# A two-layer trunk in split precision: modulation chunks in two buffer slots, an earlier gate, two more seven-product pairs

## The chip, the cores and the metric

The kernel runs on one core of one Trainium2 chip. Its time is the device time of one execution in microseconds; the median of three runs counts. Separately, the hardware profiler took one execution; all views of the profile below come from that one. The engines are called by their short names: PE is TensorE, DVE VectorE, ACT ScalarE, POOL GpSimd, SP the engine whose queue issues the loads.

## The reference

Two layers work on a latent stream of 256 tokens and a context stream of 256 tokens, both 1024 wide, with shared weights. All is float32.

```
for i in range(2):
    ml = split(silu(c)     @ w_ada[i] + b_ada[i], 9)   # shift, scale, gate for three sub-layers
    mc = split(silu(c_ctx) @ w_ada[i] + b_ada[i], 9)
    x = x + 0.5 * g1 * swiglu(modulate(rmsnorm(x, norm_w[0]), sh1, sc1), w_ffn1_in, w_ffn1_out)
    x = x + g2 * token_mixer(modulate(rmsnorm(x, norm_w[1]), sh2, sc2))
    x = x + 0.5 * g3 * swiglu(modulate(rmsnorm(x, norm_w[2]), sh3, sc3), w_ffn2_in, w_ffn2_out)
return rmsnorm(x_latent, final_norm_w)

swiglu(h, w_i, w_o) = (silu(h @ w_i[:, :2816]) * (h @ w_i[:, 2816:])) @ w_o
modulate(h, shift, scale) = h * (1 + scale) + shift
```

`x` stands for both streams, each with its own modulation (`ml` or `mc`). The token mixer projects once into 1952 columns, runs latent attention with 8 heads on one part and a gated convolution of width 3 on the other, and projects the two back together. In the second layer the context stream is needed only as keys and values, so that everything after that layer's mixer, and the last modulation vectors (5 to 8), are for the latent stream alone.

## The kernel before

**Number format.** Each matrix product is made of three PE products (`mm3`, L228, L229, L230): high part of the weight by high part of the data, high by low, low by high. A weight arrives as a 512 KB load into `wraw` (three buffers). ACT casts it to the high part `whi` (L234), DVE subtracts that from the raw weight to get the low part `wlo` (L235); each has five buffers. Products accumulate in four PSUM buffers named `mm`; four more, tag `psn`, serve norms and special sums.

**Residual and norm.** `X` holds both streams transposed, features on partitions, 8 blocks of 128 features by 512 tokens. An output projection (`into_x`) makes eight blocks: each ends with a DVE operation that adds the gated product to `X` (L347), ACT squares the new `X` (L280) and DVE adds that to `acc` (L284). The first five blocks take both streams in one 512-column product, the last three take each stream apart, so that the norm of the context stream can start while the latent stream is still being made. The norm is a chain: PE sums `acc` over partitions (`psn_s`, L244), DVE adds epsilon, POOL takes the power, PE spreads the result over partitions (`psn_r`, L252), DVE multiplies into `t` (L302), and `h` comes out as a high part on ACT (L303) and a low part on DVE (L304). Before the last FFN, PE covers this chain with products on `ax`, the not yet normalised data; those products go to `psf` and `mm` and are scaled afterwards.

**FFN.** 2816 hidden features are 22 pairs (one gate tile and one up tile of 128 features), run as two halves of 11 pairs, each half followed by its output projection. A regular pair (`gated`) is 48 matmuls of 512 columns. A fast pair (`gated_fast`) makes the same two products with seven instead of eight block products, in 84 matmuls of 256 columns, and needs more additions on DVE before and after. `FAST` lists the fast pairs of the first, second and third FFN. The fourth FFN (`ffn_end`) has the latent stream alone, turns the output around (tokens on partitions), and multiplies its output weights by the gate as they arrive (`wload(..., by=gb)`, L213). For that, the gate vector has to lie along the free dimension, the same on all partitions: `spread` (L532, L534) lets PE broadcast it with eight small matmuls and ACT copy it to `gb`.

**Modulation.** The modulation vectors are 18 products of a vector by a 1024 × 1024 matrix. They are not made on PE (but for the first two): the matrix is cut in chunks of 128 outputs, SP loads a chunk `wa` of 512 KB, and one DVE operation per stream multiplies it by the activated condition and sums along the row (L175), writing the products, which nobody needs, to `junk`. 128 chunks make 224 such operations. `wa` and `junk` live in pool `g`, with three slots of 512 KB, which `gb`, the fast pairs' `fg` and some mixer tiles use too. The chunks stand in a queue. `ada(n, after)` adds n to an account and issues one chunk for each whole unit; `PACE` has, for each of the first three FFNs, the n per pair and the n per joint output block. `ada_until(d, m)` issues whatever is still missing up to vector m of layer d.

**Order.** The kernel is written with a tile framework that works out a static order of all instructions on each engine from a planner's timeline, and waits between engines by semaphores. A small edit therefore moves instructions in places that the diff doesn't name. Loads go through SP in one queue.

The mixer interleaves the attention's heads with the convolution's projections; the head outputs `o` are split into `mixa` (two heads to a tile), the convolution's into `mixc`, and the output projection takes `mixc` first, the `mixa` of the last heads last.

Of the kernel before, what the change touches and what calls it, by code (L numbers as in the profile page):

```python
# [18 lines left out]
P = 128  # L19
# [3 lines left out]
TT = 2 * T  # L23
# [32 lines left out]
LEAD = 1  # L56
EARLY_AT = (1, 1, 2, 2, 3, 3)
NT1 = 3
PACE = ((0.85, 1.75), (0.8, 1.7), (0.9, 1.75))
MIX_PACE = 0  # L60
FAST = ((8, 10, 13, 15, 17, 19), (6, 8, 10, 13, 15, 17, 19), (6, 8, 10, 13, 15, 17, 19))


@with_exitstack
def tile_kernel(ctx: ExitStack, tc: tile.TileContext, xT, ctxT, cT, cR, w_ada, b_ada, norm_w,
                f1i, f1o, f2i, f2o, f2r, w_in, qn_w, kvn_w, w_uq, w_ukv, conv_w, w_out, fin_w,
                qtab, out):
    nc = tc.nc
# [35 lines left out]
    ident = const.tile([P, P], F32, name="ident")  # L104
# [64 lines left out]
    def ada_chunk(d, m, ct):  # L169
        wt = slot("g", "wa")  # L170
        load(wt, w_ada[d, m, ct])
        md = mods[d][m]
        for s in needed(d, m):
            junk = slot("g", "junk")
            nc.vector.scalar_tensor_tensor(junk, wt, 1.0, scb[:, s, :], ALU.mult, ALU.mult,  # L175
                                           accum_out=md[:, s, ct:ct + 1])
        if ct == NKT - 1:
            for s in needed(d, m):
                nc.vector.tensor_tensor(md[:, s, :], md[:, s, :], ba[:, d, m, :], ALU.add)
                if m % 3 == 1:  # L180
                    nc.vector.scalar_tensor_tensor(md[:, s, :], md[:, s, :], 1.0, nw[:, d, m // 3, :],
                                                   ALU.add, ALU.mult)
                if m in (2, 8):
                    nc.vector.tensor_scalar_mul(md[:, s, :], md[:, s, :], 0.5)
# [329 lines left out]

            into_x(d, gate, streams, lambda i: wo[d, half, i], hid, nxt if half else None, pace)

    def ffn_end(d, wi, wr, gate, nrm):


        ada_until(d, gate)  # L520
        parts = [(tt, h) for tt in range(2) for h in range(2)]
        gb = slot("g", "gb")
        fwb = slot("g", "fwb")
        load(fwb, fin_w.broadcast_to([P, D]))
        xt, acc = {}, {}

        def spread(h, after):

            ps = mmtile((0, TT))
            for k in range(4):  # L530
                with tc.issue_after(after.ins):
                    nc.tensor.matmul(ps[:, k * P:(k + 1) * P], mod(d, gate, 1, 4 * h + k).broadcast_to([P, P]), ident,  # L532
                                     start=True, stop=True)
            nc.scalar.copy(gb[:, h * TT:(h + 1) * TT], ps)  # L534

        def turn_x(part, tag, after):
            tt, h = part
# [17 lines left out]
        hid, w = {}, {}  # L555
        for j in range(NPAIR):
            hid[j], end = gated(d, wi, j, nrm, [1])
            if j == 1:
                for h in range(2):
                    spread(h, last_mm[0])  # L560
            if j == 2:
                for part in parts:
                    acc[part] = psn.tile([P, TT], F32, tag="psn", name="pse")
            if 6 <= j < 9:
                turn_x(parts[j - 6], ("cv", "cv", "qf")[j - 6], last_mm[0])
            k = j - LAG
            if 0 <= j - 1:
                w[j - 1] = wload(wr[j - 1], WCH, by=gb)
            if 0 <= k < NPAIR - TAIL:
                for part in parts:  # L570
                    gather(part, k, hid[k], w[k])
# [33 lines left out]
    def mixer(d, H, last, nxt):  # L605
# [212 lines left out]
                attend(*units[i - 2], st2.pop(i - 2))  # L818
        for _ in steps:
            pass  # L820

        pooled[0] = False
        ada_until(d, 5)
        order = (4, 5, 6, 7, 0, 1, 2, 3)
        into_x(d, 5, qs, lambda i: w_out[d, i], [MIX[k] for k in order], nxt, (0, 0 if last else MIX_PACE))


    ends = {}
# [43 lines left out]
    for d in range(DEPTH):  # L872
# [2 lines left out]
        ffn(d, f1i, f1o, 2, prev, [0, 1], nrm, PACE[2 * d], FAST[2 * d])  # L875
        qs = [1] if last else [0, 1]
        H, nrm = nrm.H, Norm(d, 2, qs)
        mixer(d, H, last, nrm)
        prev, nrm = nrm, None if last else Norm(d + 1, 0, qs)
        if last:  # L880
            ffn_end(d, f2i, f2r, 8, prev)
        else:
            ffn(d, f2i, f2o, 8, prev, qs, nrm, PACE[1], FAST[1])

# [78 lines left out]
```

## Time and profile before

| | |
|---|---|
| median of three runs | 1666.20 us (1666.19 to 1667.68) |
| profiled execution's own time | 1667.98 us |
| its span in the trace | 1666.2 us |
| mean granted PE clock | 0.993 |
| PE busy | 1620.8 us, 97% |
| DVE busy | 1233.5 us, 74% |
| ACT busy | 681.0 us, 41% |
| read from HBM | 246.28 MB, 148 GB/s over the span |

How to read the views quoted below. A row of a timeline has its start in us from the start of the span, its duration, the engine, the source line, the operation, the tile written and the tiles read, the shape, how many instructions the row joins, and in brackets how long the engine had been idle and what ended that. A row of a table of stretches has the stretch, its length, the busy time and number of instructions for PE, PE's weight loads, DVE, ACT and POOL, the granted PE clock, the busy share of the DMA engines and their GB/s. A row of the waits has the waiting engine, tile and line, an arrow to what it waited for, the sum of the idle time, how many times, and the longest. A row of the groups has line, engine, operation, tiles, shape and count, then the busy time and mean ns of one, then the idle time ahead of them and what ended most of it. A row of the loads has the tiles, the queue, the count, the size and the median us from issue to landing. The stages lie so: the start and the first FFN to 390 us, first mixer to 607 us, second FFN to 966 us, the second layer's FFN to 1340 us, last mixer to 1465 us, last FFN to the end.

### The profile page before, as it was taken

How to read it: one execution, taken by the hardware profiler on the slowest of the kernel's cores; microseconds unless marked ns; L12 is line 12 of the kernel's file. 1: busy time of each engine (PE TensorE's matmuls, PEld its weight loads, DVE VectorE, ACT ScalarE, POOL GpSimd, SP SyncE). 2: the span in 40 equal slices, each digit the busy share in tenths (PEclk: the TensorE clock that was granted, in tenths of full speed). 3: DMA queues.
4: the chain of work that ended last, by engine and by line, in shares of the span. 5: the costliest groups of instructions: out<-in, count | busy, mean ns of one | idle time of the engine just before them, and what ended most of it. 6: DMA issues, size and time to landing. Idle time of an engine off the chain costs nothing.

```text
span 1666.2 us, 24512 instructions
## 1 busy us (share of the span) xinstructions
PE 1620.8 (97%) x9605; PEld 1418.5 (85%) x9605; DVE 1233.5 (74%) x2049; ACT 681.0 (41%) x1097; POOL 58.1 (3%) x65
## 2 busy tenths in 40 slices
PE   6999999999999999999999999999999999999998
PEld 5889888888877688888898888988998998989997
DVE  5597788787477778878887779876675578766665
ACT  4433224323476354331243244331343257744443
POOL 0000000001111000000000000000000011100000
PEclk9999999999999999999999999999999999999999
DMA  9335555553222333346445533456345333345653
GB/s 374 134 114 164 190 168 160 171 180 100 74 75 71 126 102 114 128 163 203 152 142 186 166 106 113 149 198 230 127 152 196 116 97 126 119 143 182 189 168 123
DMA packets 73363, 249.70 MB, mean 150 GB/s; under 512 B 8736, under 2 KB 12960, under 8 KB 73248
## 3 DMA queue, kind: packets, MB, share of 16 engines
q1 hardware_dynamic: 72960, 247.62, 45.1%
q8 instruction: 75, 1.23, 0.3%
q10 hardware_dynamic: 288, 0.52, 0.1%
q14 instruction: 40, 0.33, 0.1%
HBM read 246.28 MB, written 1.05 MB: 148 GB/s over the span
## 4 chain that ended last, share of the span: by engine, by line
PE 79%; DMA 9%; DVE 7%; issue 3%; ACT 2%; SPq 0%; POOL 0%; DVEq 0%; POOLq 0%; ACTq 0%
PE mm L228 21%; PE mm L229 21%; PE mm L230 21%; DMA wa<-in_w_ada 6%; DMA wraw<-in_f2r 2%; DVE junk L175 2%; DVE wlo L235 2%; PE psg L228 2%; PE psg L230 2%; PE psg L229 2%; PE pso L784 1%; PE pst L771 1%; PE pse L228 1%; PE pse L229 1%; PE pse L230 1%
## 5 line engine op out<-in xcount | busy, mean ns | idle before, releaser
L234 ACT CAST whi<-wraw 128x1024 fp32r<-128x1024 f32 (+1 forms) x345 | 350.8, 1022 | 636.6 <-PE mm L229 341.7
L228 PE MATMUL mm<-h,whi 128*128 128x256 f32 (+1 forms) x1488 | 504.5, 343 | 5.1 <-ACT whi L234 3.1
L229 PE MATMUL mm<-h,whi 128*128 128x256 f32 (+1 forms) x1488 | 503.8, 340 | 4.1 <-DVE h L304 3.8
L230 PE MATMUL mm<-h,wlo 128*128 128x256 f32 (+1 forms) x1488 | 502.7, 339 | 0.1
L235 DVE TENSOR_TENSOR wlo<-wraw,whi 128x1024 fp32r<-128x1024 f32 (+1 forms) x345 | 408.8, 1190 | 112.9 <-ACT whi L234 105.8
L228 PEld LDWEIGHTS mm<-h,whi 128*128 128x128 f32 x1488 | 281.3, 191 | 43.4 <-issue 7.3
L175 DVE SCALAR_TENSOR_TENSOR junk<-wa,scb 128x1024 f32<-128x1024 f32 x224 | 267.1, 1223 | 63.0 <-DMA wa<-in_w_ada 62.0
L229 PEld LDWEIGHTS mm<-h,whi 128*128 128x128 f32 x1488 | 283.6, 191 | 35.2 <-DVE h L304 5.4
L230 PEld LDWEIGHTS mm<-h,wlo 128*128 128x128 f32 x1488 | 283.5, 191 | 30.5 <-DVE wlo L235 0.3
L230 PE MATMUL mm<-hid,wlo 128*128 128x512 f32 (+1 forms) x627 | 224.4, 358 | 0.0
L229 PE MATMUL mm<-hid,whi 128*128 128x512 f32 (+1 forms) x627 | 224.2, 358 | 0.0
L228 PE MATMUL mm<-hid,whi 128*128 128x512 f32 (+1 forms) x627 | 223.1, 358 | 0.0
L229 PEld LDWEIGHTS mm<-hid,whi 128*128 128x128 f32 x627 | 120.0, 191 | 16.7
L228 PEld LDWEIGHTS mm<-hid,whi 128*128 128x128 f32 x627 | 120.0, 191 | 16.7
L230 PEld LDWEIGHTS mm<-hid,wlo 128*128 128x128 f32 x627 | 119.9, 191 | 16.6
L347 DVE SCALAR_TENSOR_TENSOR X<-mm,mod,X 128x256 f32<-128x256 f32 x120 | 53.4, 478 | 38.5 <-PE mm L230 38.1
L234 ACT CAST hid<-sg 128x512 fp32r<-128x512 f32 (+1 forms) x88 | 49.0, 561 | 47.3 <-DVE sg L386 30.5
L213 DVE TENSOR_TENSOR wraw<-wraw,gb 128x1024 f32<-128x1024 f32 x22 | 26.9, 1224 | 49.8 <-DMA wraw<-in_f2r 47.0
L235 DVE TENSOR_TENSOR hid<-sg,hid 128x512 fp32r<-128x512 f32 (+1 forms) x88 | 54.0, 613 | 10.1 <-ACT hid L234 10.1
L280 ACT ACTIVATE sq<-X 128x256 f32<-128x256 f32 x63 | 25.4, 414 | 86.3 <-DVE X L347 80.2
L222 POOL TENSOR_TENSOR wlo<-wraw,whi 128x512 fp32r<-128x512 f32 x18 | 25.1, 1414 | 794.0 <-ACT whi L219 794.0
L386 DVE TENSOR_TENSOR sg<-sg,mm 128x512 f32<-128x512 f32 (+1 forms) x65 | 38.0, 584 | 18.5 <-PE mm L230 18.2
(236 smaller groups left out, 2213.5 us busy)
## 6 DMA issues: line engine op xcount, KB each, us to landing
wa<-in_w_ada SPq DMA_DIRECT2D x128, 512.0 KB, 4.0
wraw<-in_f1i SPq DMA_DIRECT2D x88, 512.0 KB, 3.6
wraw<-in_f2i SPq DMA_DIRECT2D x88, 512.0 KB, 4.0
wraw<-in_f1o SPq DMA_DIRECT2D x44, 512.0 KB, 3.8
wraw<-in_w_in SPq DMA_DIRECT2D x32, 512.0 KB, 3.5
wraw<-in_f2o SPq DMA_DIRECT2D x22, 512.0 KB, 3.6
wraw<-in_f2r SPq DMA_DIRECT2D x22, 512.0 KB, 4.6
waf<-in_w_ada SPq DMA_DIRECT2D x16, 512.0 KB, 8.2
```

Of the source, the lines that this page charges most:

```text
L175: nc.vector.scalar_tensor_tensor(junk, wt, 1.0, scb[:, s, :], ALU.mult, ALU.mult, accum_out=md[:, s, ct:ct + 1])
L213: nc.vector.tensor_tensor(raw, raw, by, ALU.mult)
L222: nc.gpsimd.tensor_tensor(w[1][:, c], raw[:, c], f32(w[0][:, c]), ALU.subtract)
L228: nc.tensor.matmul(ps, w[0], x[0], start=start, stop=False)
L229: nc.tensor.matmul(ps, w[0], x[1], start=False, stop=False)
L230: last_mm[0] = nc.tensor.matmul(ps, w[1], x[0], start=False, stop=stop)
L234: nc.scalar.copy(hi, src)
L235: return eng.tensor_tensor(lo, src, f32(hi), ALU.subtract)
L280: nc.scalar.activation(sq, xs, AF.Square)
L347: end = nc.vector.scalar_tensor_tensor(xm, pt[:, s * T - c[0]:(s + 1) * T - c[0]], mod(d, gate, s, m), xm, ALU.mult, ALU.add)
L386: nc.vector.tensor_tensor(sg, sg, ps[1], ALU.mult)
L771: end = nc.tensor.transpose(pt[:, kt * P:(kt + 1) * P], pr[:, kt * P:(kt + 1) * P], ident)
```

## The change

- A chunk's second product is written in place: for the latent stream (the second operation of a chunk, or its only one) the products go over the chunk itself, no longer to a `junk` of its own. A chunk with two operations then holds two slots of `g` instead of three, one with a single operation one instead of two.
- The pace of the first FFN goes from 0.85 chunks a pair and 1.75 a joint output block to 0.9 and 2.15.
- The second and third FFN get eight fast pairs instead of seven: 6, 8, 10, 12, 14, 16, 18, 20. The first keeps its six.
- The last gate is spread at the end of the last mixer, before its output projection, instead of after the second pair of the last FFN. `gb` is handed to `ffn_end`.
- `MIX_PACE`, which was 0, is gone.

PE has 72 matmuls more in the program, DVE 22 instructions more, ACT 6; SP's loads are as many.

```
-PACE = ((0.85, 1.75), (0.8, 1.7), (0.9, 1.75))
-MIX_PACE = 0
-FAST = ((8, 10, 13, 15, 17, 19), (6, 8, 10, 13, 15, 17, 19), (6, 8, 10, 13, 15, 17, 19))
+PACE = ((0.9, 2.15), (0.8, 1.7), (0.9, 1.75))
+FAST = ((8, 10, 13, 15, 17, 19), (6, 8, 10, 12, 14, 16, 18, 20), (6, 8, 10, 12, 14, 16, 18, 20))
...
         for s in needed(d, m):
-            junk = slot("g", "junk")
+            junk = slot("g", "junk") if s == 0 else wt
             nc.vector.scalar_tensor_tensor(junk, wt, 1.0, scb[:, s, :], ALU.mult, ALU.mult,
                                            accum_out=md[:, s, ct:ct + 1])
...
+    def spread(col):
+        to = slot("g", "gb")
+        for h in range(2):
+            ps = mmtile((0, TT))
+            for k in range(4):
+                nc.tensor.matmul(ps[:, k * P:(k + 1) * P], col(4 * h + k).broadcast_to([P, P]), ident,
+                                 start=True, stop=True)
+            nc.scalar.copy(to[:, h * TT:(h + 1) * TT], ps)
+        return to
+
-    def ffn_end(d, wi, wr, gate, nrm):
-        ada_until(d, gate)
+    def ffn_end(d, wi, wr, gb, nrm):
         parts = [(tt, h) for tt in range(2) for h in range(2)]
-        gb = slot("g", "gb")
...
-        def spread(h, after):
-            ps = mmtile((0, TT))
-            for k in range(4):
-                with tc.issue_after(after.ins):
-                    nc.tensor.matmul(ps[:, k * P:(k + 1) * P], mod(d, gate, 1, 4 * h + k).broadcast_to([P, P]), ident,
-                                     start=True, stop=True)
-            nc.scalar.copy(gb[:, h * TT:(h + 1) * TT], ps)
...
-            if j == 1:
-                for h in range(2):
-                    spread(h, last_mm[0])
...
         for _ in steps:
             pass
+        gb = None
+        if last:
+            ada_until(d, 8)
+            gb = spread(lambda kt: mod(d, 8, 1, kt))
...
-        into_x(d, 5, qs, lambda i: w_out[d, i], [MIX[k] for k in order], nxt, (0, 0 if last else MIX_PACE))
+        into_x(d, 5, qs, lambda i: w_out[d, i], [MIX[k] for k in order], nxt)
+        return gb
```

The order of the instructions moves at three places that matter below. Names carry a running number, which differs between the two kernels; the line numbers of the changed kernel are smaller by one to four.

**DVE at the end of the first FFN**, where the last blocks of the context stream are added to `X` and squared sums to `acc0`. Before:

```order
L347 SCALAR_TENSOR_TENSOR X_109<-mm_3258,mod0_2_126,X_109 128x256
L179 TENSOR_TENSOR mod0_6_130<-mod0_6_130,ba_104 128x8
L284 TENSOR_TENSOR acc0_666<-acc0_666,sq_3305 128x256
L175 SCALAR_TENSOR_TENSOR junk_3254,mod0_7_131<-wa_3252,scb_102 128x1024
L175 SCALAR_TENSOR_TENSOR junk_3256,mod0_7_131<-wa_3252,scb_102 128x1024
L347 SCALAR_TENSOR_TENSOR X_109<-mm_3308,mod0_2_126,X_109 128x256
L284 TENSOR_TENSOR acc0_666<-acc0_666,sq_3349 128x256
L347 SCALAR_TENSOR_TENSOR X_109<-mm_3352,mod0_2_126,X_109 128x256
L235 TENSOR_TENSOR wlo_3604<-wraw_3601,whi_3603 128x1024
L284 TENSOR_TENSOR acc0_666<-acc0_666,sq_3393 128x256
```

After:

```order
L346 SCALAR_TENSOR_TENSOR X_109<-mm_3297,mod0_2_126,X_109 128x256
L174 SCALAR_TENSOR_TENSOR wa_3237,mod0_7_131<-wa_3237,scb_102 128x1024
L283 TENSOR_TENSOR acc0_666<-acc0_666,sq_3338 128x256
L174 SCALAR_TENSOR_TENSOR junk_3244,mod0_7_131<-wa_3242,scb_102 128x1024
L346 SCALAR_TENSOR_TENSOR X_109<-mm_3341,mod0_2_126,X_109 128x256
L174 SCALAR_TENSOR_TENSOR wa_3242,mod0_7_131<-wa_3242,scb_102 128x1024
L234 TENSOR_TENSOR wlo_3593<-wraw_3590,whi_3592 128x1024
L283 TENSOR_TENSOR acc0_666<-acc0_666,sq_3382 128x256
```

The last chunk's second product, now in place (`wa` is written and read), stands between the last `X` and the last `acc0`. Counted over the whole order, 82 chunk products precede the end of the first FFN before and 94 after; 14 and 2 stand in the first mixer.

**PE at the end of the first mixer**, from the last head's `pso` to the first product that uses that head's `mixa` (`mixa_5094` before, `mixa_5083` after). Before:

```order
L228 MATMUL mm_5285<-mixa_4804,whi_5288 128x512
L784 MATMUL pso_5161<-pT_5139,v_3982 64x256 x2
L784 MATMUL pso_5161<-pT_5139,v_3983 64x256 x2
L229 MATMUL mm_5285<-mixa_4804,whi_5288 128x512
L230 MATMUL mm_5285<-mixa_4804,wlo_5289 128x512
L228 MATMUL mm_5172<-mixa_5094,whi_5175 128x512
```

After:

```order
L780 MATMUL pso_5150<-pT_5128,v_3971 64x256 x2
L780 MATMUL pso_5150<-pT_5128,v_3972 64x256 x2
L228 MATMUL mm_5235<-mixa_4207,whi_5238 128x512
L229 MATMUL mm_5235<-mixa_4207,wlo_5239 128x512
L227 MATMUL mm_5235<-mixa_4498,whi_5238 128x512
...
L227 MATMUL mm_5274<-mixa_4793,whi_5277 128x512
L228 MATMUL mm_5274<-mixa_4793,whi_5277 128x512
L229 MATMUL mm_5274<-mixa_4793,wlo_5278 128x512
L227 MATMUL mm_5161<-mixa_5083,whi_5164 128x512
```

Between the last `pso` and that first use stand two other matmuls before, and nineteen after.

**ACT at the start of the last FFN**, from the end of the gate's spread, or of the last squares, to the second FFN weight that the stage casts after the norm. `R` is the norm's factor, `wb` a column of the `ax` products. `wraw_13844`, `wraw_13923` before and `wraw_13834`, `wraw_13913` after are gated output weights, the others are input weights. Before:

```order
L534 COPY gb_13681<-mm_13832 128x512
L534 COPY gb_13681<-mm_13838 128x512
L290 COPY R_13646<-psn_r_13643 128x256
L234 CAST whi_13847<-wraw_13844 128x1024
L234 CAST whi_13853<-wraw_13851 128x1024
L234 CAST whi_13859<-wraw_13857 128x1024
L303 ACTIVATE h_13648<-t1_13649,mod1_6_139 128x256
L303 ACTIVATE h_13648<-t1_13653,mod1_6_139 128x256
...
L303 ACTIVATE h_13648<-t1_13657,mod1_6_139 128x256
...
L376 ACTIVATE f_13799<-f_13799,wb_13773 128x256
L234 CAST whi_13926<-wraw_13923 128x1024
```

After:

```order
L233 CAST whi_13837<-wraw_13834 128x1024
L279 ACTIVATE sq_13630<-X_109 128x256
L269 ACTIVATE ax_13632<-X_109,mod1_7_140 128x256
L233 CAST whi_13843<-wraw_13841 128x1024
L233 CAST whi_13849<-wraw_13847 128x1024
L289 COPY R_13649<-psn_r_13646 128x256
L233 CAST whi_13916<-wraw_13913 128x1024
L372 COPY wb_13701<-psf_13699 128x1
...
L302 ACTIVATE h_13651<-t1_13652,mod1_6_139 128x256
L302 ACTIVATE h_13651<-t1_13656,mod1_6_139 128x256
L302 ACTIVATE h_13651<-t1_13660,mod1_6_139 128x256
L233 CAST whi_13938<-wraw_13936 128x1024
```

The two input weights and the first two gated ones are now cast ahead of the first `h`, and the next input weight (`whi_13938`) directly behind the third `h`; before, a gated weight (`whi_13926`) stood ahead of the next input weight.

More of the change, by code (lines that the diff above doesn't have):

```diff
@@ L877, in tile_kernel @@
         H, nrm = nrm.H, Norm(d, 2, qs)
-        mixer(d, H, last, nrm)
+        gb = mixer(d, H, last, nrm)
         prev, nrm = nrm, None if last else Norm(d + 1, 0, qs)
         if last:
-            ffn_end(d, f2i, f2r, 8, prev)
+            ffn_end(d, f2i, f2r, gb, prev)
         else:
```

## The prediction

> **What bounds the kernel now.** I read the engines' busy time first, then what TensorE (PE) waits for, then those waits in their stretches.
>
> ```profile
> PE 1620.8 (97%) x9605; PEld 1418.5 (85%) x9605; DVE 1233.5 (74%) x2049; ACT 681.0 (41%) x1097; POOL 58.1 (3%) x65
> engine line waited for: us in total, times, longest us
> PE psn_s L244 <- DVE acc L284: 6.4, 4, 2.6
> PE mm L229 <- DVE h L304: 3.8, 5, 1.7
> PE mm L228 <- ACT whi L234: 3.1, 1, 3.1
> PE mm L228 <- ACT mixa L234: 2.2, 1, 2.2
> PE mm L229 <- DVE mixc L235: 0.7, 1, 0.7
> ```
>
> PE is busy for 1620.8 of 1666.2 us. So a gain has two sources only: less work for PE, or fewer of the few waits, all of a few microseconds. The waits lie at the seams between stages. There the granted clock matters too, because some of them are followed by a stretch at half speed. A table of stretches shows this (length; busy us of PE, weight loads, VectorE, ScalarE, GpSimd; clock; DMA share; GB/s):
>
> ```profile
> 387.50:390.90 3.40, 1.76 (x16) 1.56 (x14) 2.78 (x5) 2.67 (x5) 0.73 (x1) 1.00 0.00 0
> 390.90:394.30 3.40, 3.40 (x17) 3.40 (x18) 1.77 (x3) 1.38 (x2) 2.65 (x3) 0.50 0.59 178
> 578.70:582.10 3.40, 1.84 (x8) 1.53 (x9) 1.19 (x3) 0.79 (x2) 0.74 (x1) 1.00 0.44 146
> 964.40:967.80 3.40, 1.42 (x12) 1.43 (x13) 3.28 (x6) 2.42 (x5) 0.00 (x0) 0.99 0.24 71
> 967.80:971.20 3.40, 3.40 (x19) 3.40 (x18) 2.16 (x5) 0.73 (x1) 0.70 (x1) 0.50 0.85 265
> 1476.40:1479.80 3.40, 0.41 (x2) 0.30 (x3) 3.40 (x7) 2.51 (x5) 0.00 (x0) 0.99 0.28 112
> 1479.80:1486.60 6.80, 6.50 (x24) 5.63 (x23) 6.32 (x12) 2.25 (x6) 0.00 (x0) 0.50 0.43 154
> ```
>
> PE idle for 3.40 − 1.76 = 1.64 us in a stretch is followed by 3.40 us at clock 0.50; idle for 3.40 − 1.84 = 1.56 us (at 578.70) it is not. I take about 1.6 us of idle per stretch as the limit. A half-speed stretch costs half its length: 1.7 us at 390.90 and 967.80, 3.4 us at 1479.80.
>
> The Trainium skill ("TensorE: Matmul & The Clock Gate", section "Why this matters for your kernels") asks for idle gaps above about 3 us before the clock falls. The trace disagrees: 1.64 us were enough. By the page the second seam below has no clock to win, and my sum would end 1.7 us higher.
>
> **Term 1: two more pairs with seven products.** A regular pair is 48 matmuls of 512 columns, a fast one 84 of 256.
>
> ```profile
> 697.70 0.39 PE L228 MATMUL mm<-h,whi 128*128 128x512 f32 x1
> 699.74 0.39 PE L228 MATMUL mm<-h,whi 128*128 128x512 f32 x1
> 702.53 0.28 PE L228 MATMUL mm<-h,whi 128*128 128x256 f32 x1
> 704.93 0.28 PE L230 MATMUL mm<-ts,wlo 128*128 128x256 f32 x1
> 1184.00:1226.00 42.00, 42.00 (x266) 38.17 (x265) 32.74 (x46) 17.02 (x23) 0.00 (x0) 1.00 0.44 151
> ```
>
> The first two rows are 9 issues apart: 2.04 / 9 = 0.2267 us per wide matmul. The next two are 20 apart: 0.120 us per narrow one. So 48 × 0.2267 = 10.88 us becomes 84 × 0.120 = 10.08 us: 0.80 us less per pair, **−1.6** for two. A fast pair gives VectorE more to do. In the last row, four pairs alternately fast and regular, VectorE is busy for 32.74 of 42 us and PE never idles, so that is hidden; with 9.26 us free per four pairs, two fast pairs next to each other (18 and 20 are not) would still fit. If that cover is gone, the term is 0; with narrow matmuls a little quicker than this, −2.4.
>
> The same skill page (section "Back-to-back issue gap") gives columns / 2.4 GHz + 2.5 ns, 215.8 and 109.2 ns. By it a pair would save 1.19 us, two 2.4, and the sum would be 0.8 lower; the rows, slower for both widths, decide.
>
> **Term 2: tail of the first mixer.** A modulation chunk is a 512 KB load and one or two VectorE operations of 1.22 us. By the order, 82 of these stand before the end of the first FFN and 14 more in the mixer; with the new pace it is 94 and 2. So 12 × 1.22 = 14.7 us of VectorE leave the mixer.
>
> ```profile
> L175 DVE SCALAR_TENSOR_TENSOR junk<-wa,scb 128x1024 f32<-128x1024 f32 x224 | 267.1, 1223 | 63.0 <-DMA wa<-in_w_ada 62.0
> 572.06 1.23 DVE L175 SCALAR_TENSOR_TENSOR junk<-wa,scb 128x1024 f32<-128x1024 f32 x1 [2.29 <-DMA wa<-in_w_ada]
> 564.84 0.50 PE L229 MATMUL mm<-mixc,whi 128*128 128x512 f32 x1 [0.70 <-DVE mixc L235]
> 579.80 0.40 ACT L234 CAST mixa<-o 64x256 fp32r<-64x256 f32 x1 [1.35 <-DVE o L791]
> 580.26 1.19 PE L228 MATMUL mm<-mixa,whi 128*128 128x512 f32 x4 [2.20 <-ACT mixa L234]
> ```
>
> VectorE stood 2.29 us at one chunk for its DMA, and behind it the last heads' work came late: PE waited 0.70 us for `mixc` and 2.20 us for `mixa`, 2.90 together. Without the chunks these operations run as their inputs arrive; PE's new order also has nineteen other matmuls between the last head's `pso` and the first use of its `mixa`. I take **−2.7**, from −2.9 to 0 (the wait is PE's own latency of the last head and stays).
>
> **Term 3: first FFN to first mixer.** The same 12 operations go into the first FFN; what they cost is at its end, where the order shows one more of them, in place, between the last `X` and the last `acc0`.
>
> ```profile
> 384.51 1.23 DVE L175 SCALAR_TENSOR_TENSOR junk<-wa,scb 128x1024 f32<-128x1024 f32 x1 [1.00 <-DMA wa<-in_w_ada]
> 388.17 0.48 DVE L347 SCALAR_TENSOR_TENSOR X<-mm,mod,X 128x256 f32<-128x256 f32 x1
> 390.38 0.60 PE L244 MATMUL psn_s<-mean,acc 128*128 128x1 f32 x4 [1.64 <-DVE acc L284]
> ```
>
> PE waits 1.64 us for `acc` now. One chunk operation more is 1.22 us, of which some hides behind the block still on PE: **+0.9**, wait about 2.5 us; the half-speed stretch is there already. Bounds −0.5 (the load's 1.00 us goes) and +2.0 (a load is late too). In the body of the stage the operations are hidden; the rival below says from where on not.
>
> **Term 4: second FFN to second layer.** Chunks now hold two of the three `g` slots, so the next load can start before the last one's second operation.
>
> ```profile
> 960.51 1.23 DVE L175 SCALAR_TENSOR_TENSOR junk<-wa,scb 128x1024 f32<-128x1024 f32 x1 [1.08 <-DMA wa<-in_w_ada]
> 964.17 0.48 DVE L347 SCALAR_TENSOR_TENSOR X<-mm,mod,X 128x256 f32<-128x256 f32 x1
> 966.38 0.61 PE L244 MATMUL psn_s<-mean,acc 128*128 128x1 f32 x4 [2.60 <-DVE acc L284]
> ```
>
> VectorE lost 1.08 us to a chunk's load just ahead of the last `X` and `acc`; PE's 2.60 us become 1.5. That is −1.1, and 1.5 is under the limit of 1.6, so the half-speed stretch (1.7) should go: the two make −2.8. The margin is a tenth of a microsecond, so I take **−2.0**; bounds −2.8 and 0.
>
> **Term 5: last mixer to last FFN.** Here the gate was spread, and everything multiplied by it waited.
>
> ```profile
> 1465.22 1.95 PE L532 MATMUL mm<-ident,mod 128*128 128x128 f32 x16
> 1476.10 1.21 DVE L213 TENSOR_TENSOR wraw<-wraw,gb 128x1024 f32<-128x1024 f32 x1
> 1477.34 1.99 ACT L234 CAST whi<-wraw 128x1024 fp32r<-128x1024 f32 x2 [0.89 <-DVE wraw L213]
> 1479.39 0.39 PE L228 MATMUL mm<-h,whi 128*128 128x256 f32 x1 [3.11 <-ACT whi L234]
> 1480.89 0.79 PE L228 MATMUL pse<-whi,hid 128*128 128x512 f32 x1 [0.29 <-ACT hid L234]
> ```
>
> PE waited 3.11 us because ScalarE's next weight cast stood behind a cast of a gated weight whose multiplication came only at 1476.10. Now the gate is there before the seam, two multiplications stand ahead of the first `h`, and the cast that PE needs comes behind three `h` with no gated weight between. The 3.11 + 0.29 = 3.40 us shrink, but not to nothing: the fourth `h` and the first `hid` still queue behind VectorE's splits, and I leave 1.2 us of them. **−2.2**. The spread itself (1.95 us) moves and costs PE the same in the mixer. Bounds: −6.8 (all 3.40, and the half-speed stretch with it) and +1.9 (nothing won, the spread holding up the last heads).
>
> **At nothing:** the in-place write is the same VectorE operation on the same shape, and the table has an in-place neighbour at the same price; its cover is not needed. The removed mixer pace was zero.
>
> ```profile
> L213 DVE TENSOR_TENSOR wraw<-wraw,gb 128x1024 f32<-128x1024 f32 x22 | 26.9, 1224 | 49.8 <-DMA wraw<-in_f2r 47.0
> ```
>
> **Sum:** −1.6 − 2.7 + 0.9 − 2.0 − 2.2 = −7.6 us. The profiled execution took 1667.98 us, with 1.8 outside its span of 1666.2; the terms are differences inside the span, so I take them off the median of the runs, 1666.2: **1658.6 us**. The forecast's own range is 1656 to 1662.
>
> **Rivals.** *The last seam goes entirely.* If PE's idle there falls under the limit, the two half-speed stretches (3.4 us) go as well: 1655.2. For it: half of the waits removed would leave no stretch near 1.6 us. Against: VectorE was busy 6.32 of 6.80 us behind the seam, so waits can spread.
>
> *The waits only move.* The cover at the seams is the same three engines; a wait taken from one operation ends at the next. Then the fast pairs and half of the mixer's tail remain: −1.6 − 1.4 = −3.0, 1663.2. For it: the second `h` and `acc` waits are in the list as well as the ones named. Against: term 2 takes work away and does not move it to a seam.
>
> *Slower: the chunks starve the first FFN.* In its output blocks PE needs 11 × 3 × 0.2267 = 7.48 us each, and the new pace asks 2.15 chunks per block, one per 3.48 us. With two slots each and three in all, a chunk takes about half of its load plus its first operation.
>
> ```profile
> wa<-in_w_ada SPq DMA_DIRECT2D x128, 512.0 KB, 4.0
> waf<-in_w_ada SPq DMA_DIRECT2D x16, 512.0 KB, 8.2
> ```
>
> With a landing of 4.0 us that is (4.0 + 1.22) / 2 = 2.6 us, enough. It decides from 2 × 3.48 − 1.22 = 5.7 us on, because the chunk's operation then sits in VectorE's order ahead of the `X` that frees PE's accumulator. The kernel has seen 8.2 us, when everything loaded at once. At 6.6 us each of some 28 chunks costs 0.43 us, 12 in all: 1666.2 − 7.6 + 12 = 1671. Against: the blocks' own weights are a light load.
>
> *The change doesn't do what it says:* the slots bring no earlier load because the sync queue is in order; that is inside the second rival.
>
> **How the numbers follow.** Forecast 0.50, last seam gone 0.15, waits only move 0.23, slower 0.12. A measurement of this kernel tells 0.2% from no change, 3.3 us: faster is below 1662.9, slower above 1669.5. Faster: 0.48 of the forecast's 0.50, all of 0.15, 0.07 of 0.23: 0.70. Same: 0.02 + 0.16 = 0.18. Slower: 0.12. The range runs from 1653 (last seam gone, narrow matmuls at the lower bound) to 1667 (the moved waits with the seams' upper bounds); the slower rival lies outside.
>
> **What would show it.** Term 1: 72 matmuls more and no new PE wait in the second and third FFN. Term 2: no wait for `mixa` or `mixc` in the first mixer's tail. Term 3: a wait for `acc` near 2.5 us at the first seam. Term 4: clock 1.00 behind the second. Term 5: no wait for `whi` at the last. I am wrong if PE waits for `mm` buffers in the first FFN's blocks, or if a stretch at 0.50 stands where none was: the grid of the stretches against the seams can cost or give 1.7 us each.

## The result

The changed kernel takes **1648.24 us** (median of four runs, 1647.50 to 1648.49), the kernel before 1666.2 (1661.82 to 1667.68 with the run beside it): a ratio of 0.9896, 95% interval 0.9877 to 0.9914. It is 18.0 us faster, where 7.6 were forecast, and lies outside the range of 1653 to 1667. The direction was right and the size was not. The profiled execution's own time went from 1667.98 to 1648.40 us, its span from 1666.2 to 1646.6; the terms are compared on these spans.

The head of the page of the changed kernel, and its two groups of chunk operations (`wa<-wa` is the product written in place):

```profile
span 1646.6 us, 24595 instructions
PE 1612.0 (98%) x9677; PEld 1415.4 (86%) x9677; DVE 1248.0 (76%) x2071; ACT 688.4 (42%) x1103; POOL 57.6 (3%) x65
L174 DVE SCALAR_TENSOR_TENSOR wa<-wa,scb 128x1024 f32<-128x1024 f32 x128 | 155.2, 1217 | 0.6
L174 DVE SCALAR_TENSOR_TENSOR junk<-wa,scb 128x1024 f32<-128x1024 f32 x96 | 117.5, 1224 | 9.0 <-DMA wa<-in_w_ada 8.0
wa<-in_w_ada SPq DMA_DIRECT2D x128, 512.0 KB, 4.4
```

The in-place product costs the same as the other. But DVE's idle time ahead of chunk products fell from 63.0 to 9.6 us, that on the chunks' loads from 62.0 to 8.0, although a load now takes 4.4 us to land instead of 4.0: so it must be issued earlier. And PE has 72 matmuls more in the program but is busy for less time: of the four half-speed stretches in the program's body, those at the seams of terms 3, 4 and 5 are gone. The waits of PE:

```profile
engine line waited for: us in total, times, longest us
PE mm L228 <- DVE h L303: 3.6, 5, 1.7
PE psn_s L243 <- DVE acc L283: 2.1, 2, 1.2
PE pse L227 <- ACT hid L233: 1.7, 1, 1.7
PE mm L227 <- ACT h L302: 1.3, 2, 1.0
```

The waits for `whi` (3.1), `mixa` (2.2) and `mixc` (0.7) are gone; that for `acc` went from 6.4 to 2.1 us, that for `hid` grew from 0.3 to 1.7.

Where the time went by stage is read from PE's timeline; the rows mark where one stage ends and the next begins. Changed kernel:

```profile
387.19 0.50 PE L243 MATMUL psn_s<-mean,acc 128*128 128x1 f32 x4
443.54 0.39 PE L227 MATMUL psv<-whi,ckvn 128*128 128x512 f32 x1
591.86 0.50 PE L243 MATMUL psn_s<-mean,acc 128*128 128x1 f32 x4
965.11 0.61 PE L243 MATMUL psn_s<-mean,acc 128*128 128x1 f32 x4 [1.21 <-DVE acc L283]
1354.82 0.47 PE L227 MATMUL psv<-whi,ckvn 128*128 128x512 f32 x1
1449.71 0.28 PE L243 MATMUL psn_s<-mean,acc 128*128 128x1 f32 x2
```

The kernel before has the same places at 390.38 (shown above) and here:

```profile
448.57 0.39 PE L228 MATMUL psv<-whi,ckvn 128*128 128x512 f32 x1
601.33 0.50 PE L244 MATMUL psn_s<-mean,acc 128*128 128x1 f32 x4
979.42 0.60 PE L244 MATMUL psn_s<-mean,acc 128*128 128x1 f32 x4 [1.20 <-DVE acc L284]
1369.87 0.47 PE L228 MATMUL psv<-whi,ckvn 128*128 128x512 f32 x1
1463.85 0.28 PE L244 MATMUL psn_s<-mean,acc 128*128 128x1 f32 x2
```

| stretch (to this row) | before, us | after, us | difference | what was forecast for it |
|---|---|---|---|---|
| first FFN and its seam, to `psv` | 448.57 | 443.54 | −5.03 | +0.9 (term 3) |
| first mixer, to `psn_s` | 152.76 | 148.32 | −4.44 | −2.7 (term 2) |
| second FFN and its seams | 378.09 | 373.25 | −4.84 | −2.8 (term 4, half of term 1) |
| third FFN, start of last mixer | 390.45 | 389.71 | −0.74 | −0.8 (half of term 1) |
| last mixer | 93.98 | 94.89 | +0.91 | +1.95 (the spread, within term 5) |
| last seam and last FFN | 202.35 | 196.89 | −5.46 | −4.15 (the rest of term 5's −2.2) |

The differences add up to −19.6 us. The clock has its part in them: the half-speed stretches between the first FFN and the last add up to 20.5 us before (3.4, 6.8, 3.4 and 6.8) and to 6.8 after, and half of that difference, 6.8 us, is time gained.

Behind the first two seams the clock now stays at full speed (stretches of the changed kernel, columns as before; the first two rows at the end of the first FFN, the next two of the second, the last two at the start of the second FFN, where the stretch at half speed is still there):

```profile
385.00:388.00 3.00, 3.00 (x28) 3.00 (x27) 1.48 (x3) 1.14 (x3) 2.25 (x2) 1.00 0.53 175
388.00:391.40 3.40, 3.40 (x31) 3.40 (x30) 1.62 (x2) 1.57 (x2) 1.14 (x2) 1.00 0.45 151
953.00:956.40 3.40, 3.40 (x31) 3.40 (x31) 1.95 (x4) 1.22 (x2) 0.70 (x1) 1.00 0.59 213
956.40:959.80 3.40, 3.40 (x31) 3.40 (x30) 2.66 (x6) 2.26 (x5) 0.00 (x0) 1.00 0.48 164
596.50:599.90 3.40, 1.47 (x11) 1.06 (x9) 2.72 (x6) 2.62 (x5) 0.00 (x0) 1.00 0.40 157
599.90:606.70 6.80, 6.08 (x28) 6.08 (x29) 5.90 (x16) 3.60 (x6) 0.70 (x1) 0.50 0.21 77
```

### The profile page after: what moved, and what is told of

Its sections match the earlier page's. It is cut to its first block, busy times and chain, and to the rows that moved or that the text cites. A ratio compares the mean times of both kernels' runs of the same rounds, so it can differ in the third digit from the quotient of the medians.

```text
span 1646.6 us, 24595 instructions
## 1 busy us (share of the span) xinstructions
PE 1612.0 (98%) x9677; PEld 1415.4 (86%) x9677; DVE 1248.0 (76%) x2071; ACT 688.4 (42%) x1103; POOL 57.6 (3%) x65
## 3 DMA queue, kind: packets, MB, share of 16 engines
q8 instruction: 76, 1.25, 0.3%
## 4 chain that ended last, share of the span: by engine, by line
PE 95%; DVE 2%; ACT 1%; issue 1%; DMA 1%; POOL 0%; SPq 0%; POOLq 0%; DVEq 0%
PE mm L227 25%; PE mm L228 25%; PE mm L229 25%; PE psg L229 2%; PE psg L228 2%; PE psg L227 2%; PE pso L780 1%; PE pse L227 1%; PE pse L228 1%; PE pse L229 1%; PE pst L767 1%; PE mme L227 1%; PE mme L229 1%; PE mme L228 1%; PE psn_s L243 1%
## 5 line engine op out<-in xcount | busy, mean ns | idle before, releaser
L233 ACT CAST whi<-wraw 128x1024 fp32r<-128x1024 f32 (+1 forms) x349 | 354.6, 1021 | 669.1 <-PE mm L228 418.3
L234 DVE TENSOR_TENSOR wlo<-wraw,whi 128x1024 fp32r<-128x1024 f32 (+1 forms) x349 | 414.3, 1191 | 135.5 <-ACT whi L233 129.4
L228 PE MATMUL mm<-h,whi 128*128 128x256 f32 (+1 forms) x1472 | 495.9, 338 | 3.9 <-DVE h L303 3.6
L227 PE MATMUL mm<-h,whi 128*128 128x256 f32 (+1 forms) x1472 | 496.0, 341 | 1.8 <-ACT h L302 1.3
L229 PE MATMUL mm<-h,wlo 128*128 128x256 f32 (+1 forms) x1472 | 494.3, 337 | 0.0
L227 PEld LDWEIGHTS mm<-h,whi 128*128 128x128 f32 x1472 | 277.8, 190 | 38.7 <-issue 7.3
L228 PEld LDWEIGHTS mm<-h,whi 128*128 128x128 f32 x1472 | 280.0, 190 | 33.7 <-DVE h L303 5.4
L229 PEld LDWEIGHTS mm<-h,wlo 128*128 128x128 f32 x1472 | 279.8, 190 | 28.9
L174 DVE SCALAR_TENSOR_TENSOR wa<-wa,scb 128x1024 f32<-128x1024 f32 x128 | 155.2, 1217 | 0.6
L174 DVE SCALAR_TENSOR_TENSOR junk<-wa,scb 128x1024 f32<-128x1024 f32 x96 | 117.5, 1224 | 9.0 <-DMA wa<-in_w_ada 8.0
L227 PE MATMUL mm<-ts,whi 128*128 128x256 f32 x176 | 49.8, 283 | 0.0
L228 PE MATMUL mm<-ts,whi 128*128 128x256 f32 x176 | 49.8, 283 | 0.0
```

What stands on the lines that cost most here:

```text
L227: nc.tensor.matmul(ps, w[0], x[0], start=start, stop=False)
L228: nc.tensor.matmul(ps, w[0], x[1], start=False, stop=False)
L229: last_mm[0] = nc.tensor.matmul(ps, w[1], x[0], start=False, stop=stop)
L233: nc.scalar.copy(hi, src)
L234: return eng.tensor_tensor(lo, src, f32(hi), ALU.subtract)
```

## The experiments

Two theories stood for the missed 10 us. **A:** the slots end DVE's waits for chunk loads, and those waits were what made `acc` late at two seams; the pace only works because of the slots. **B:** the pace is what matters, and the slots merely make room for it.

### Each part alone

```
slots only:   junk = slot("g", "junk") if s == 0 else wt
pace only:    PACE = ((0.9, 2.15), ...)
fast only:    FAST = (..., (6, 8, 10, 12, 14, 16, 18, 20), (6, 8, 10, 12, 14, 16, 18, 20))
gate only:    gb = spread(...) at the end of the last mixer
```

> The kernel before with the in-place second product alone: a chunk holds two slots of g. Theory A (VectorE's waits for chunk loads, 62.0 us in all before and 8.0 after, are what made acc late at the seams; the slots remove them): waits for chunk loads fall below 15 us, the wait for acc at the end of the first FFN (1.64 us) and at the end of the second FFN (2.60 us) go, each with its half-speed stretch of 3.4 us, and part of the mixer's tail: -3.3 -4.3 -1.5 and about -1.5 of the small waits, some 1655.5 us. Theory B (the pace is what matters, the slots only make room for it): the 14 chunk products stay in the first mixer and their waits with them, the seams change little: 1661 to 1666 us.

> The kernel before with the first FFN's pace 0.9 and 2.15 alone; a chunk still holds three slots. Theory A: VectorE's waits for chunk loads in the first FFN grow from 25 us to 30 us or more, the mixer's tail is freed (-3.4), the seam at the end of the first FFN gets worse by 1 to 3 us: 1663 to 1667 us. Theory B: nearly the whole gain of the first FFN and the mixer, -9, 1657 us.

> The kernel before with the fifteenth and sixteenth fast pair alone (8 instead of 7 in the second and third FFN). Both theories: 0.8 us less in each of the two FFNs, 1664.6 us; the third FFN's length 344.9 becomes 344.1 us. If the other order of VectorE matters, up to 3 us either way at the end of the second FFN.

> The kernel before with the last gate spread in the mixer alone. Theory A and B alike, if the places are independent: last FFN -4.8 us (1.4 us of waits and 3.4 us of half speed less), last mixer +0.9, norm -0.6: 1661.7 us. If the gain at this seam came from the other edits instead: no change, 1666 us.

| kernel | median, us | range of its runs | ratio to before, 95% |
|---|---|---|---|
| slots only | 1658.60 | 1656.58 to 1660.77 | 0.9938 (0.9916 to 0.9960) |
| pace only | 1674.73 | 1670.19 to 1675.60 | 1.0034 (1.0015 to 1.0052) |
| fast only | 1663.66 | 1659.59 to 1666.75 | 0.9976 (0.9956 to 0.9996) |
| gate only | 1662.23 | 1658.67 to 1667.22 | 0.9969 (0.9950 to 0.9988) |

The slots alone make the kernel 0.62% faster by the ratio, some 10 of the 18 us (7.7 by the medians of this set, in which the kernel before took 1666.31); in the profiled execution `psv` comes at 443.20 us (before 448.57, changed kernel 443.54). The chunk products of that run, and PE's waits:

```profile
L175 DVE SCALAR_TENSOR_TENSOR wa<-wa,scb 128x1024 f32<-128x1024 f32 x128 | 155.4, 1219 | 0.9
L175 DVE SCALAR_TENSOR_TENSOR junk<-wa,scb 128x1024 f32<-128x1024 f32 x96 | 117.5, 1224 | 8.0 <-DMA wa<-in_w_ada 7.1
```

```profile
PE mm L228 <- ACT whi L234: 3.1, 1, 3.1
PE mm L228 <- ACT mixa L234: 2.9, 1, 2.9
PE psn_s L244 <- DVE acc L284: 2.1, 2, 1.2
```

The 62.0 us of waits for chunk loads are 7.1, and `acc` is down to the 2.1 us that the changed kernel has. That is theory A's mechanism, though not its time: 1658.60 lies between A's 1655.5 and B's 1661. And part of my reasoning falls: PE still waits 2.9 us for `mixa` in the mixer's tail, though DVE no longer waits for a load there. The way from the last head's `pso` to its `mixa`, with the slots alone and then in the changed kernel:

```profile
570.54 1.08 PE L784 MATMUL pso<-pT,v 128*64 128x256 f32 x8
574.02 0.40 ACT L234 CAST mixa<-o 64x256 fp32r<-64x256 f32 x1 [1.35 <-DVE o L791]
565.47 1.08 PE L780 MATMUL pso<-pT,v 128*64 128x256 f32 x8
568.96 0.40 ACT L233 CAST mixa<-o 64x256 fp32r<-64x256 f32 x1 [1.34 <-DVE o L787]
```

It takes 3.9 us in both, as in the kernel before (576.31 to 580.20), and no chunk product stands in it in any of the three. What differs is PE's order. With the slots alone the first product on that `mixa` comes directly behind `pso`; in the changed kernel nineteen other matmuls stand between and cover the rest of the way. So the wait comes neither from the chunks' loads nor from their products at that place, but from what PE has left to do beside it.

The pace alone is 0.34% slower by the ratio, some 6 us (8.4 by the medians), and slower than A had expected. Chunk products of the first FFN (a stretch of the group view, before and pace alone), then DVE and PE of the pace-alone run at one place in it:

```profile
L175 DVE SCALAR_TENSOR_TENSOR junk<-wa,scb 128x1024 f32<-128x1024 f32 x82 | 97.1, 1222 | 25.0 <-DMA wa<-in_w_ada 25.0
```

```profile
L175 DVE SCALAR_TENSOR_TENSOR junk<-wa,scb 128x1024 f32<-128x1024 f32 x90 | 106.6, 1222 | 29.8 <-DMA wa<-in_w_ada 29.5
```

```profile
259.81 1.23 DVE L175 SCALAR_TENSOR_TENSOR junk<-wa,scb 128x1024 f32<-128x1024 f32 x1 [0.91 <-DMA wa<-in_w_ada]
260.96 1.22 DVE L175 SCALAR_TENSOR_TENSOR junk<-wa,scb 128x1024 f32<-128x1024 f32 x1
262.11 2.35 DVE L235 TENSOR_TENSOR wlo<-wraw,whi 128x1024 fp32r<-128x1024 f32 x2
263.38 0.58 PE L230 MATMUL mm<-ts,wlo 128*128 128x256 f32 x1 [3.49 <-DVE wlo L235]
```

The split that PE needs stands behind two chunk products, the first of which waits for its load; PE waits 3.49 us. `psv` comes at 462.69 us, 14.1 later than before. Half-speed stretches ahead of `psv` add up to 17.1 us in this run, against 3.4 in the kernel before, so 6.8 of the 14.1 us are the clock. The first mixer, on the other hand, takes 148.27 us, as in the changed kernel. So the mixer's gain belongs to the pace, with which PE's order in the mixer's tail changes too (the way from `pso` to `mixa` is 3.9 us here as well, and covered). And the pace is bought in the first FFN, at 14 us with three slots and at nothing with two.

The fast pairs and the gate alone gave about what was expected; the third FFN, from the norm's `psn_r` to the next `psn_s`, went from 344.9 to 344.25 us with the former, and the last FFN lost its long wait with the latter.

### Each part undone

The second set takes one part at a time out of the changed kernel.

> The changed kernel with the in-place second product undone: a chunk holds three slots again, the faster pace stays. Theory A (the pace needs the slots: with three slots VectorE waits for each chunk's load): the first FFN's output blocks wait on VectorE as with the pace alone, 62.6 - 1.6 + 390 = first seam 10 us or more later, total the pace-alone 1674.7 less about 2 for the fast pairs and 4 for the gate: 1668 us. Rival, the parts add up independently: 1648.2 + 7.7 (what the slots gave alone) = 1656 us.

> The changed kernel with the first FFN's pace put back to 0.85 and 1.75. Theory A: 14 chunk products are in the first mixer again, its length goes from 148.3 to about 153.5 us (3.4 us of waits in the tail), the first FFN stays: 1653 us. Rival, the parts add up independently (the pace alone cost 8.4): 1640 us.

> The changed kernel with the last gate's spread put back into the last FFN. If the gain there belongs to the spread: the wait for a weight cast behind a gated weight (3.1 us) and the half-speed stretch behind it are back, the last mixer is 0.9 us shorter: 1652.3 us. If the other edits carried it: 1648 us.

> The changed kernel with seven fast pairs again in the second and third FFN. Term 1 as predicted: 0.8 us per pair, 1648.2 + 1.6 = 1649.8 us, the third FFN 344.9 instead of 344.1 us. If the order of the second FFN's end moves with it: up to 3 us more.

| changed kernel without | median, us | range of its runs | ratio to before, 95% |
|---|---|---|---|
| the slots | 1670.29 | 1665.62 to 1673.66 | 1.0031 (1.0017 to 1.0044) |
| the pace | 1652.84 | 1652.28 to 1653.44 | 0.9933 (0.9914 to 0.9951) |
| the gate's move | 1651.22 | 1649.58 to 1652.00 | 0.9921 (0.9905 to 0.9938) |
| the fast pairs | 1649.50 | 1647.87 to 1650.95 | 0.9900 (0.9882 to 0.9918) |

All four came out near the time expected of theory A or of the part's own gain, and the additive rival is out for both slots (1656 expected) and pace (1640). Without the slots the whole change is slower than the kernel before: about 22 us of its time hang on that one line. Without the pace the first mixer takes 152.26 us instead of 148.32, with the wait in its tail:

```profile
574.80 1.19 PE L227 MATMUL mm<-mixa,whi 128*128 128x512 f32 x4 [2.85 <-ACT mixa L233]
```

Without the gate's move, the wait and the half speed at the last seam are back as they were:

```profile
1464.35 0.58 PE L228 MATMUL mm<-h,whi 128*128 128x256 f32 x1 [3.11 <-ACT whi L234]
```

```profile
1460.29:1463.70 3.41, 0.95 (x8) 0.75 (x7) 3.41 (x8) 1.92 (x4) 0.00 (x0) 1.00 0.62 234
1463.70:1470.53 6.83, 5.89 (x20) 5.02 (x21) 6.83 (x13) 3.32 (x8) 0.00 (x0) 0.50 0.48 150
```

The two fast pairs come out at 1.3 us here (1649.50 − 1648.24), forecast at 1.6. But the two kernels ran in different sets, between which the kernel before went from 1666.20 to 1664.71 us, and their ranges overlap; by the ratios the difference is 0.7 us. The total doesn't show this gain; the third FFN does.

### The clock, and what is still to be had

The changed kernel has one half-speed stretch left in its body, at 599.90. Repeated copies of the norm's spread, which nothing reads, keep PE at work there (four, then eight of them):

```
             R = rstd(self.sums[s], D, T, "n")
+            if (self.d, self.i, s) == (0, 2, 0):
+                W = psn.tile([P, TT], F32, tag="psn", name="psw")
+                for t in range(WARM):
+                    nc.tensor.matmul(W[:, t % 4 * P:(t % 4 + 1) * P], last_r[0][:, 0:1].broadcast_to([P, P]), ident, start=True, stop=True)
```

> The changed kernel with four matmuls more between the first mixer's norm of the context stream and the first product on it: they repeat the norm's spread into a buffer that nothing reads, 0.97 us of TensorE work in a wait of 0.99 us. Theory (a stretch with over about 1.6 us of TensorE idle brings the half clock, whatever TensorE did in the rest): the idle there falls from 2.65 to about 1.7 us, spread over two stretches, the half-speed stretch of 6.83 us at 599.9 goes, 3.4 us less: 1644.8 us. Rival (the stretch is brought by the longest single wait, 1.66 us, which stays): no change, 1648.2 us, or 1 us more.

> As the run with four matmuls more at the first mixer's norm, with eight. TensorE is then busy for 1.94 us of the 2.65 it waits, and the wait for the low part of h that follows should shrink from 1.66 to about 0.7 us at the same end. Theory (idle per stretch decides): no half-speed stretch there in any execution, 1644.8 us and a narrower spread than with four. Rival (the matmuls hold up the first product on h, and what follows on the other engines): later by up to 1 us, 1646.7 us.

With four: **1645.74 us** (1644.47 to 1647.62), ratio 0.9891 (0.9873 to 0.9908). With eight: 1646.84 us (1646.41 to 1647.20), ratio 0.9884 (0.9868 to 0.9901). The seam with four:

```profile
596.00:599.40 3.40, 2.04 (x16) 1.63 (x14) 2.84 (x6) 2.61 (x5) 0.00 (x0) 1.00 0.45 157
599.40:602.80 3.40, 3.00 (x24) 2.96 (x25) 3.40 (x10) 1.31 (x3) 0.20 (x1) 1.00 0.54 154
602.80:606.20 3.40, 3.40 (x31) 3.40 (x30) 3.21 (x9) 2.01 (x5) 0.67 (x1) 1.00 0.00 0
```

The half speed is gone in this execution, though the longest wait of 1.66 us is still there; the rival that this wait alone brings it is out. The stretch called second FFN above took 370.38 us in it instead of 373.25. (Of the run's other three executions two had a lower mean clock, 0.998 and 0.997 against 0.999, so some half speed was left in them.) By the medians four and eight are 2.5 and 1.4 us below the changed kernel; by the ratios, which compare each with the kernel before in its own set, 0.8 and 2.0. With intervals this wide, that either is faster than the changed kernel is likely, not shown. With eight there was another half-speed stretch, at a seam that none of these edits touches:

```profile
959.90:963.30 3.40, 2.20 (x17) 1.83 (x16) 3.40 (x8) 1.65 (x4) 0.00 (x0) 1.00 0.46 131
963.30:966.70 3.40, 3.40 (x19) 3.40 (x18) 2.02 (x6) 0.96 (x2) 0.70 (x1) 0.51 0.27 105
```

PE was idle for 1.20 us only. My limit of 1.6 us is not a limit; see the last section.

The last two runs add fast pairs to the kernel with eight.

```
warm8_f9:     FAST = ((8, 10, 13, 15, 17, 19), (6, 8, 10, 11, 13, 15, 17, 19, 21), (6, 8, 10, 11, 13, 15, 17, 19, 21))
warm8_f899:   FAST = ((8, 10, 11, 13, 15, 17, 19, 21), (6, 8, ..., 21), (6, 8, ..., 21))
```

> Eight matmuls more at the seam, and nine fast pairs (6, 8, 10, 11, 13, 15, 17, 19, 21) in the second and third FFN; 10 and 11 have an output projection between them. If VectorE's slack still covers a fast pair: 0.8 us less per FFN, 1.6 below the run with eight matmuls alone, 1643.2 us. If not, waits for wlo or eg appear in the third FFN: 1645 us or more.

> As before, and eight instead of six fast pairs (8, 10, 11, 13, 15, 17, 19, 21) in the first FFN, where VectorE also has 94 chunk products. If its slack covers them: 1.6 us less again, 1641.6 us. If VectorE is full there (waits for acc, wlo or sg in the first FFN): 1645 us or more.

They took 1651.08 us (ratio 0.9914, 0.9893 to 0.9935) and 1666.59 us (1.0009, 0.9996 to 1.0021): 4.2 us slower than eight matmuls alone, and 19.8. In the first of them the ninth fast pair does save its 0.7 us in the third FFN (343.56 us from `psn_r` to `psn_s` instead of 344.27), so DVE's slack covers it inside the stage. The second FFN and its seams lose 2.8 us, because at the end PE now waits 2.15 and 1.68 us for `h` (a half-speed stretch follows there in both runs). Another 1.25 us lie ahead of the first mixer's `psv`, where this edit changes nothing: a half-speed stretch at 396.1, which the run with eight doesn't have. Pair 21 is the last one ahead of the output projection; that its additions on DVE push back what follows was not tried apart. In the second, DVE falls behind in the first FFN. Of PE's waits over the whole execution, the 3.0 us for `fg`, 2.3 of those for `sg` and 4.2 of those for `h` lie in that stage and at its end, where chunk products still stand on DVE:

```profile
PE mm L228 <- ACT h L309: 7.6, 3, 4.2
PE mm L228 <- ACT sg L391: 3.5, 2, 2.3
PE mm L228 <- DVE fg L492: 3.0, 1, 3.0
```

```profile
243.16 1.22 DVE L175 SCALAR_TENSOR_TENSOR wa<-wa,scb 128x1024 f32<-128x1024 f32 x1
243.39 0.36 PE L228 MATMUL mm<-h,whi 128*128 128x256 f32 x1 [3.05 <-DVE fg L492]
```

A fast pair's addition `fg` stood behind chunk products, and PE's buffers were free only after it. So two fast pairs more in the first FFN cost 15 us, where one more in the third gains 0.7.

## Why the prediction was wrong

**Term 1 (−1.6) was right.** The third FFN is 0.75 us shorter with its one more fast pair (344.88 to 344.13 us from `psn_r` to `psn_s`), and the slots alone leave it at 344.90.

**Term 3 (+0.9) failed, and this was the largest miss.** I priced the added chunk products and one operation more between the last `X` and the last `acc0`, and took the stage's body as hidden. That operation does stand there. But I had quoted 62.0 us of waits for chunk loads and asked only at one seam what the two-slot chunk takes of them. In the first FFN alone they were 25.0 us; they are 3.9 now. With them went PE's 1.64 us wait for `acc` at the seam, two waits inside the stage that I left out (0.65 us at 113.4 and 0.83 at 258.9, 3.12 with the seam's), and the half-speed stretch behind: −5.0 us. The slots alone show it, with `psv` at 443.20. The operation that I priced is hidden, because DVE is now ahead at that point.

**Term 4 (−2.0) named the right cause and kept too much of the wait.** The 2.60 us at `acc` became nothing, not 1.5. Less the fast pair, the stage gained 4.0 us, beyond the bound of −2.8. The 1.08 us ahead of the last `X` was only the last of several chunk waits in a row, which had all made DVE late.

**Term 2 (−2.7) was mis-sized, and its cause wrong for the larger wait.** The mixer is 4.4 us shorter. The waits of 0.70 and 2.20 us went, with 0.53 us of two others, and about 1 us in stretches that count as busy. It was not the 2.29 us wait for a load that held up `mixa`: with the slots alone that wait is gone and PE waits longer than before, 2.9 us. Nor did chunk products hold it up, since none stands between the last `pso` and its `mixa`: this way takes 3.9 us with 14 chunk products in the mixer and with two. That is the latency of the last head, which I had named as the reason for a gain of 0. It stayed, and the nineteen matmuls, which I mentioned second, cover it. That PE's order has them there only with the faster pace is what the runs show; why, they don't. The smaller wait, for `mixc`, fits the prediction: in the kernel before two chunk products stand right ahead of it on DVE (561.82 and 562.96, `mixc` at 564.10).

**Term 5 (−2.2) had the right mechanism and the wrong rest.** The wait for `whi` went whole, 3.11 us. The wait for `hid` grew from 0.29 to 1.71 us, about the 1.2 us that I left standing, but smaller waits stand beside it (0.5 us for `f`, 0.4 for `h`, 0.3 for `r`): in all, PE's waits from this seam on fell from 4.0 to 2.9 us, by 1.1 and not by 2.2. Both half-speed stretches behind the seam went too, 3.4 us, which I had only in a rival at 0.15. The spread cost the last mixer 0.91 us, not its full 1.95; with that the two stages gained 4.55 us, most of it clock.

**The rivals.** "The last seam goes entirely" came true beside the forecast's other terms, but by luck as far as its condition goes: it asked for less than 1.6 us of idle in a stretch, and there were 1.71 (last section). "The waits only move" was wrong: the waits named here are gone and only some 2 us turned up elsewhere (1.4 of it at `hid`). "The chunks starve the first FFN" is a real mechanism, but for three slots: the pace alone and the change without the slots are both slower than before, and the place is the split of a fast pair's weights, not the output blocks' accumulators as I had it. With two slots it doesn't come near.

**The sum.** The prediction says that with no clock to win at the second seam the sum would end 1.7 us higher. That doesn't fit the sum: term 4 was taken at −2.0 between −1.1 without the clock and −2.8 with it, so it would end 0.9 higher. And the low end of the range, 1653, doesn't follow from the two things named for it, which give 1655.2 − 0.8 = 1654.4. Neither touches the miss.

What the sum lacked in kind: I added terms seam by seam, each from the wait that ended last there. An edit that removes a wait from 224 operations in three stages is worth more than what one seam shows of it, because what ends at a seam is the sum of the delays before it.

## What to carry to other kernels

Where the profile has tens of microseconds of waits of one kind on an engine that is "not the bottleneck", follow them to the next point where the bottleneck engine waits for that engine: there they come out as a sum, and one buffer less in use per item may end nearly all of them (62.0 us became 8.0). A higher pace for background work is to be tested with the buffers that it needs, since the same pace made the kernel before 0.34% slower and, with the slots, was worth 4.6 us (0.3%). Short waits at seams are worth more than their length where the clock drops behind them. And before a wait is put down to what an engine did earlier, compare the chain that it ends between two runs: that of `mixa` was equally long with and without the change, and only the work beside it differed.

## What the runs showed of the hardware

All half-speed stretches of an execution lie on one grid. In the kernel before they start at 390.9, 609.4, 967.8 and 1479.8 us; the distances from the first, 218.5, 576.9 and 1088.9 us, are 64, 169 and 319 times 3.413 us. The Trainium skill ("TensorE: Matmul & The Clock Gate", section "What's actually happening") tells of a free-running window of 3413 ns, and the traces agree. So whether a wait brings half speed depends on where the grid cuts it. One wait shows it: ahead of the latent stream's norm at the end of the second FFN, PE waits 1.20 or 1.21 us for `acc` in many of the runs. Half speed follows within 2 us without the pace (969.5), without the fast pairs (965.9) and with eight matmuls (963.3), and not in the changed kernel or with the slots alone. Part of what the clock gave the change in one execution is therefore chance.

And idle time by the profile isn't what counts. In the changed kernel, this stretch on the grid has 1.71 us of idle and no half speed behind it:

```profile
1463.47:1466.88 3.41, 1.70 (x9) 1.25 (x8) 3.41 (x8) 1.24 (x4) 0.00 (x0) 1.00 0.11 44
1466.88:1470.29 3.41, 3.41 (x30) 3.41 (x29) 1.92 (x5) 1.26 (x3) 0.00 (x0) 1.00 0.02 5
```

The stretch with 1.20 us of idle shown for eight added matmuls does have it. The former holds matmuls of 256 and 512 columns, the latter also four of one column (`psn_s`), which together read as busy for some 0.6 us. Counted by their columns at the spacing of the wide matmuls (0.2267 us for 512), the former has 1.4 us of work and the latter 1.2. Counted so over the traces of all 14 profiled executions, the stretches that brought half speed had 0 to about 1.4 us, and of the thousands of others only six had less than 1.33. So by this count the limit lies near 1.3 us of columns in a stretch of 3.41. The six, from about 1.1 us up, are left open: in four of them PE shows no idle time at all, a few matmul records are missing from a trace, and no run was made to settle it. It fits with the spread of the runs, though four of each are few: in the set that they shared, the kernel before took from 1661.82 to 1667.68 us, the changed kernel, with fewer waits for the grid to cut, from 1647.50 to 1648.49.
